# The gathered token tile first through residual and queries, and 352 score columns instead of 384

## The chip, the cores and the metric

The kernel runs on one core of a Trainium2 chip. The metric is the device time of one execution in microseconds. One execution was also recorded by the hardware profiler; all rows below come from that record. PE is TensorE, DVE VectorE, ACT ScalarE, POOL GpSimd and SP SyncE, which here only issues transfers.

## The reference

One encoder block over 512 tokens of 1024 features: a mixer (convolution and pooling heads), a product-key expert layer, and a gated embedding.

```python
h = h + jnp.concatenate([y_conv, y_pool], axis=-1) @ w_o[i]
h = h + peer_ffn(rms_norm(h, g_ffn[i]), w_q[i], sub_keys[i], expert_u[i], expert_v[i])
gate = jax.nn.sigmoid(rms_norm(h, g_ple[i]) @ w_ple_gate[i])
h = h + gate * (p[i] @ w_ple_proj[i])

def peer_block(xb, w_q, sub_keys, expert_u, expert_v):   # xb: normed tokens
    q = (xb @ w_q).reshape(T, PEER_HEADS, 2, PEER_HALF)
    s = jnp.einsum('thpd,hpkd->thpk', q, sub_keys)
    sv, si = lax.top_k(s, PEER_TOPK)                      # 16 of 128, per half
    cand = sv[:, :, 0, :, None] + sv[:, :, 1, None, :]    # 256 sums per head
    top_s, pos = lax.top_k(cand.reshape(T, 8, 256), PEER_TOPK)
    gate = jax.nn.softmax(top_s)
    act = jax.nn.gelu(jnp.einsum('thkd,td->thk', expert_u[eidx], xb))
    return jnp.einsum('thk,thkd->td', gate * act, expert_v[eidx])
```

Each token uses 8 x 16 = 128 of 16384 experts; an expert has a row of 1024 floats in U and one in V.

## The kernel before, in words

The 512 tokens are four tiles of 128. Every fp32 operand is split into a high part (ACT, a copy to fp32r) and a low part (DVE, source minus high part), and each product is three matmuls (high·high, high·low, low·high: `mm3`, lines 118 to 127).

The expert layer works in two ways. The last tile (`ND`, the gathered tile) fetches the 128 U rows and 128 V rows of each token by indirect DMA on POOL (line 536; one gather brings one row for each of 128 tokens), multiplies and sums on DVE (lines 556, 560). The other three tiles (the dense ones, 384 columns) are scored against all experts: 128 U blocks of 128 experts, `score` at line 609, with a gate matrix that is zero except at the chosen experts and that PE builds from one-hot rows (`onehot`, lines 447 to 482), then a product with the 128 V blocks (`mix`).

The stages in time: mixer with w_in; residual, where four 1 MB pieces of w_o (256 columns) each serve four tiles (lines 304 to 316); norm and transposes; queries, eight 1 MB pieces of w_q each for 512 columns, followed by key scores and the first top-16 (`head`, lines 498 to 521); phase 1, U blocks 0 to 75 with the remaining top-k work, the one-hots and the first gathers (lines 626 to 640); the fused stage, where U blocks 76 to 127 are scored beside the first V mixes; the last stage with V mixes and the remaining gathers; and a tail with the embedding gate.

What sets the order: up to the end of phase 1 the framework schedules each engine's queue from its own model of durations. `MAIN_ORDER` orders the top-k tasks of the tiles in phase 1, `spent` spreads them evenly over the blocks (line 636), `G_START` and `G_RATE1` (line 640) set from which block and at what rate gathers run there. The later stages are written out by hand, with `RATES` and the rest of the gathers spread over the last stage (line 801). Pieces of weights use two buffers each for the raw load, the high part and the low part (`wraw`, `wH`, `wL`, lines 159 to 170); each loop loads and splits the next piece before it uses the present one. Each engine and each DMA queue runs in its own order.

## Time and profile before

| | us |
|---|---|
| median of 3 runs | 1453.2 (1452.3 to 1453.3) |
| profiled execution | 1454.46 |
| its span (first to last instruction) | 1452.7 |
| PE busy | 1430.8 |
| DVE busy | 1137.7 |
| ACT busy | 614.5 |
| POOL busy | 390.7 |

The profiled execution is longer than its span by 1.8 us, the time around the first and the last instruction. A busy time is the union of an engine's instructions, so overlapped matmuls are counted once. [...]

### The profile page before, as it was taken

The page shows a single profiled execution, that of the slowest core. Times are in us where ns is not written, and L with a number is a line of the kernel's source. Part 1 is how long each engine was busy: PE and PEld are TensorE (multiplying, and loading weights), DVE is VectorE, ACT ScalarE, POOL GpSimd, SP SyncE. Part 2 cuts the span into 40 slices and gives each one's busy share as a digit, 9 for nine tenths or more (in the row PEclk, how much of TensorE's full clock was granted, in tenths as well). Part 3 has the DMA queues.
Part 4 walks back from the last instruction along what each step waited for, and adds up shares of the span by engine and source line. Part 5 has one row for each costly group of instructions (what it writes and reads, how often), then busy time and mean ns, then how long its engine had stood idle before and what let it go on. Part 6 is the DMA issues. An engine that isn't in the chain of part 4 may idle for free.

```text
span 1452.7 us, 20601 instructions
## 1 busy us (share of the span) xinstructions
PE 1430.8 (98%) x7785; PEld 1271.6 (88%) x7785; DVE 1137.7 (78%) x2078; ACT 614.5 (42%) x864; POOL 390.7 (27%) x260
## 2 busy tenths in 40 slices
PE   8999999999998999999999999999999999999997
PEld 5789888999998999998999999999998888788886
DVE  5644579899998987879988778888877777776765
ACT  5321533344564665664333333333333334433354
POOL 0000000002132132125766555454443123342000
PEclk9999999999998999999999999999999999999999
DMA  8223730047688899899998999998997899998721
GB/s 302 87 90 104 242 116 30 30 164 279 227 285 268 274 316 326 262 317 347 380 349 323 375 329 339 347 339 324 346 336 273 317 334 333 335 342 324 249 70 73
DMA packets 152083, 381.38 MB, mean 263 GB/s; under 512 B 10928, under 2 KB 72112, under 8 KB 151728
## 3 DMA queue, kind: packets, MB, share of 16 engines
q1 hardware_dynamic: 72400, 211.75, 41.3%
q0 software_dynamic: 36864, 134.23, 25.3%
q10 hardware_dynamic: 42720, 34.08, 7.2%
q8 instruction: 61, 1.00, 0.3%
q14 instruction: 38, 0.31, 0.1%
HBM read 339.92 MB, written 40.11 MB: 262 GB/s over the span
## 4 chain that ended last, share of the span: by engine, by line
PE 71%; DVE 12%; DMA 7%; issue 6%; ACT 2%; POOL 1%; ACTq 1%; SPq 0%; DVEq 0%; POOLq 0%
PE o L127 11%; PE o L123 11%; PE o L125 11%; PE acc L125 6%; PE acc L123 6%; PE acc L127 6%; PE u L127 5%; PE u L123 5%; PE u L125 5%; DMA uraw<-in_u_blk 3%; DVE uL L586 2%; DMA tH<-in_w_gate 2%; POOL gr L536 1%; PE acc L191 1%; PE tp L516 1%
## 5 line engine op out<-in xcount | busy, mean ns | idle before, releaser
L536 POOL DMA_INDIRECT gr<-in_u_rows,eidx x128 | 201.1, 1571 | 652.5 <-DVE tsm L390 334.6
L536 POOL DMA_INDIRECT gr<-in_v_rows,eidx x128 | 189.4, 1480 | 285.2 <-DVE xrow L560 274.5
L125 PE MATMUL o<-vL,wH 128*128 128x512 f32 x768 | 237.2, 390 | 0.7 <-DVE vL L604 0.7
L123 PE MATMUL o<-vH,wH 128*128 128x512 f32 x768 | 237.7, 390 | 0.3 <-ACT wH L685 0.3
L127 PE MATMUL o<-vH,wL 128*128 128x512 f32 x768 | 237.3, 390 | 0.1
L598 ACT ACTIVATE vH<-vraw 128x1024 fp32r<-128x1024 f32 x128 | 135.4, 1058 | 218.3 <-PE o L127 160.8
L123 PE MATMUL acc<-xH,uH 128*128 128x384 f32 x608 | 206.6, 340 | 3.4 <-ACT uH L580 3.4
L604 DVE TENSOR_TENSOR vL<-vraw,vH 128x1024 fp32r<-128x1024 f32 x128 | 156.2, 1221 | 65.2 <-ACT vH L598 64.9
L125 PE MATMUL acc<-xL,uH 128*128 128x384 f32 x608 | 206.8, 340 | 0.0
L127 PE MATMUL acc<-xH,uL 128*128 128x384 f32 x608 | 204.7, 339 | 0.2 <-DVE uL L586 0.2
L580 ACT ACTIVATE uH<-uraw 128x1024 fp32r<-128x1024 f32 x128 | 135.3, 1058 | 100.6 <-DMA uraw<-in_u_blk 64.0
L586 DVE TENSOR_TENSOR uL<-uraw,uH 128x1024 fp32r<-128x1024 f32 x128 | 155.7, 1217 | 24.8 <-ACT uH L580 24.8
L125 PEld LDWEIGHTS o<-vL,wH 128*128 128x128 f32 x768 | 144.0, 188 | 32.3 <-DVE vL L604 1.5
L127 PEld LDWEIGHTS o<-vH,wL 128*128 128x128 f32 x768 | 143.9, 188 | 31.2 <-DVE wL L690 1.0
L560 DVE SCALAR_TENSOR_TENSOR xrow<-gr,gate,xrow 128x1024 f32<-128x1024 f32 x128 | 164.1, 1282 | 5.1 <-DMA xrow<-h_d 4.6
L123 PEld LDWEIGHTS o<-vH,wH 128*128 128x128 f32 x768 | 143.3, 188 | 27.2 <-ACT wH L685 0.7
L556 DVE SCALAR_TENSOR_TENSOR gr<-gr,xrow 128x1024 f32<-128x1024 f32 x128 | 154.3, 1218 | 4.2 <-DMA gr<-in_u_rows,eidx 4.1
L127 PE MATMUL u<-xH,uL 128*128 128x384 f32 x416 | 139.6, 336 | 0.0
L123 PE MATMUL u<-xH,uH 128*128 128x384 f32 x416 | 139.5, 335 | 0.0
L125 PE MATMUL u<-xL,uH 128*128 128x384 f32 x416 | 139.3, 335 | 0.0
L123 PEld LDWEIGHTS acc<-xH,uH 128*128 128x128 f32 x608 | 115.4, 190 | 4.1 <-ACT uH L580 4.1
L127 PEld LDWEIGHTS acc<-xH,uL 128*128 128x128 f32 x608 | 115.1, 189 | 0.8 <-DVE uL L586 0.8
(214 smaller groups left out, 2336.8 us busy)
## 6 DMA issues: line engine op xcount, KB each, us to landing
uraw<-in_u_blk SPq DMA_DIRECT2D x128, 512.0 KB, 5.2
vraw<-in_v_rows SPq DMA_DIRECT2D x128, 512.0 KB, 6.0
G_d<-stage ACTq DMA_DIRECT2D x12, 1664.0 KB, 12.8
gq<-G_d SPq DMA_DIRECT2D x26, 768.0 KB, 7.0
A_d<-a ACTq DMA_DIRECT2D x17, 768.0 KB, 6.0
aq<-A_d SPq DMA_DIRECT2D x17, 768.0 KB, 9.5
wraw<-in_w_in SPq DMA_DIRECT2D x8, 1024.0 KB, 5.8
wraw<-in_w_q SPq DMA_DIRECT2D x8, 1024.0 KB, 5.8
```

The costliest lines, as they stand in the source:

```text
L123: nc.tensor.matmul(ps, lh, rh, start=start, stop=False)
L125: nc.tensor.matmul(ps, lh, rl, start=False, stop=False)
L127: nc.tensor.matmul(ps, ll, rh, start=False, stop=stop)
L191: nc.tensor.matmul(ps, pT[:, c, t * P:(t + 1) * P], wp[hf][:, c], start=c == 0, stop=c == 1)
L516: nc.tensor.matmul(ps[:, o:o + P], qb[b][:, t * P:(t + 1) * P], keys[:, 2 * hd + b], start=True, stop=True)
L536: nc.gpsimd.indirect_dma_start(out=g, out_offset=None, in_=table, in_offset=bass.IndirectOffsetOnAxis(ap=eidx[:, k:k + 1], axis=0))
L556: ins = nc.vector.scalar_tensor_tensor(g, g, 1.0, xrow, op0=OP.mult, op1=OP.mult, accum_out=act[:, k:k + 1])
L560: ins = nc.vector.scalar_tensor_tensor(accg, g, gate3[:, k - P:k - P + 1], accg, op0=OP.mult, op1=OP.add)
L580: nc.scalar.activation(ublk[i][1], ublk[i][0], AF.Copy)
L586: nc.vector.tensor_tensor(ublk[i][2], raw, uh.bitcast(F32), op=OP.subtract)
L598: nc.scalar.activation(vblk[n][1], vblk[n][0], AF.Copy)
L604: nc.vector.tensor_tensor(vblk[n][2], raw, vh.bitcast(F32), op=OP.subtract)
```

## The change

The gathered tile goes through residual and queries alone and first. Its four pieces of w_o are loaded and split; then eight q pieces for it alternate with four o pieces for the three dense tiles; then eight q pieces come for the dense tiles. So 12 o and q pieces become 24 (`todo_w`). The low part of the last seven is made on GpSimd (`eng`). The top-k tasks of the gathered tile run in that stage instead of phase 1.

Scores take 352 columns (`TU`) instead of 384. The last 32 tokens of tile 2 get their scores from gathered U rows: 32 more gathers (`XK`), each of 32 tokens x 4 rows, on indices that four small POOL DMAs lay over 128 partitions (`index_x`). Their activations go back by four more DMAs (`actt`) and into the gate of tile 2 before its one-hots (`weigh_x`), with one scale per token (`unit_x`) that the eviction of these tokens' one-hots on DVE takes off again. The score tiles hold 1.0 in the last 32 columns. The gathers of the fused stage keep their rates; phase 1 has 64 instead of 46, the last stage 60 instead of 46.

```diff
-G_START = 10
-G_RATE1 = 0.7
+G_START = 4
+G_RATE1 = 0.9
-MAIN_ORDER = ((ND, 0, 99), (0, 0, 99), (1, 0, 99), (2, 0, 99))
+MAIN_ORDER = ((2, 0, 14), (0, 0, 99), (1, 0, 99), (2, 14, 99))
+XT = 32
+XQ = P // XT
+XK = P // XQ
+TU = TD - XT
-    iotar = consts.tile([P, 2 * OB // PR, P, PR], F16, name="iotar")
+    iotar = consts.tile([P, 2, P * PR], F16, name="iotar")
-    def split_ld(src, hi, lo):
+    def split_ld(src, hi, lo, eng=None):
         nc.scalar.activation(hi, src, AF.Copy)
-        nc.vector.tensor_tensor(lo, src, hi.bitcast(F32), op=OP.subtract)
+        (eng or nc.vector).tensor_tensor(lo, src, hi.bitcast(F32), op=OP.subtract)
+        def index_x():
...
+            for q in range(XQ):
+                nc.gpsimd.dma_start(eidx_x[q * XT:(q + 1) * XT], ex[XROWS, q * XK:(q + 1) * XK])
+        def weigh_x():
+            while todo["x"]:
+                gather(1, True)
+            g = d["g"][XROWS]
+            nc.vector.tensor_tensor(g, g, act_t[XROWS], op=OP.mult)
...
+            nc.gpsimd.dma_start(unit_d.rearrange("a n -> n a"), s)
+            nc.gpsimd.dma_start(unit_x, bass.AP(tensor=unit_d.tensor, offset=unit_d.offset, ap=[[0, P], [1, XT]]))
+                if t0 >= TU:
...
+                        nc.vector.tensor_tensor(o.rearrange("p i t -> p t i"), pv[:, :, i], unit, op=OP.mult)
+    todo_w = ([("o", n) for n in range(4)] + [("o", 0), ("q", 0), ("q", 1), ("o", 1), ("q", 2), ("q", 3), ("o", 2),
+              ("q", 4), ("o", 3), ("q", 5), ("q", 6), ("q", 7)] + [("q", hd) for hd in range(H)])
+    NX = len(todo_w) - H
+    def weights(n):
+        m = n + 1
+        if m < len(todo_w):
+            kind, i = todo_w[m]
+            got[m] = piece(w_o if kind == "o" else w_q, i * 256, 2 if kind == "q" and m < NX else 1,
+                           nc.gpsimd if m > NX else None)
+        return got.pop(n)
+    for n in range(4):
+        residual(weights(n), n, [ND])
...
+    for n in range(4, NX):
+        w = weights(n)
+        kind, i = todo_w[n]
+        if kind == "o":
+            residual(w, i, range(ND))
+        else:
+            queries_n(w, i)
...
     for hd in range(H):
+        both = projT(weights(NX + hd), xh, xl, TD)
...
+        for _ in range(3):
+            if tasks_n:
+                tasks_n.pop(0)[1]()
+        for t in (2, 0, 1):
+            heads[t](hd, s[:, t])
+        for kind, n in (("x", XK if ready else 0), ("u", P), ("v", P)):
...
-            mm3(ps[:, :TD], uh[:, c], ul[:, c], xh[:, c, :TD], xl[:, c, :TD], c == 0, c == DC - 1)
+            mm3(ps[:, :TU], uh[:, c], ul[:, c], xh[:, c, :TU], xl[:, c, :TU], c == 0, c == DC - 1)
```

The first place is the queue of SP from the w_o pieces to the last w_q piece. Before (`wraw` is a raw weight piece, `uraw` a raw U block):

```order
L160 DMA wraw<-in_w_o 128x8x256 x4
L160 DMA wraw<-in_w_q 128x8x256 x3
L327 DMA h_d<-h 128x1024 x3
L325 DMA keys<-in_keysT 128x2048
L327 DMA h_d<-h 128x1024
L193 DMA ple_d<-pleo 128x512 x2
L160 DMA wraw<-in_w_q 128x8x256
L193 DMA ple_d<-pleo 128x512 x2
L574 DMA uraw<-in_u_blk 128x1024 x2
L334 DMA xs<-in_g_ffn 128x1024
L574 DMA uraw<-in_u_blk 128x1024 x3
L160 DMA wraw<-in_w_q 128x8x256 x4
```

After, from the keys of the gathered tile (`uH<-in_keysT`) on; three rows with w_o and one with `ple_d` stand ahead of it:

```order
L550 DMA uH<-in_keysT 128x1024 x2
L174 DMA wraw<-in_w_o 128x8x256
L174 DMA wraw<-in_w_q 128x8x256
L547 DMA h_d<-h 128x1024
L553 DMA xs<-in_g_ffn 128x1024
L174 DMA wraw<-in_w_q 128x8x256
L174 DMA wraw<-in_w_o 128x8x256
L174 DMA wraw<-in_w_q 128x8x256 x2
L174 DMA wraw<-in_w_o 128x8x256
L174 DMA wraw<-in_w_q 128x8x256
L174 DMA wraw<-in_w_o 128x8x256
L174 DMA wraw<-in_w_q 128x8x256 x3
```

Twelve pieces that each served all four tiles are now followed or preceded by twelve more; o and q pieces alternate, and the keys, the row store `h_d` and the gain vector stand between them.

The second place is DVE in phase 1, around U block 50. Before (`uL` is the low part of a U block, `oh` and `gg` a one-hot pair, `gr` a gathered row's product):

```order
L586 TENSOR_TENSOR uL<-uraw,uH 128x1024
L460 TENSOR_TENSOR gg<-oh,tr 128x2048
L586 TENSOR_TENSOR uL<-uraw,uH 128x1024
L556 SCALAR_TENSOR_TENSOR gr,act<-gr,xrow 128x1024
L458 TENSOR_TENSOR oh<-iotar,tr 128x2048
L460 TENSOR_TENSOR gg<-oh,tr 128x2048
L556 SCALAR_TENSOR_TENSOR gr,act<-gr,xrow 128x1024
L458 TENSOR_TENSOR oh<-iotar,tr 128x2048
L586 TENSOR_TENSOR uL<-uraw,uH 128x1024
L556 SCALAR_TENSOR_TENSOR gr,act<-gr,xrow 128x1024
L460 TENSOR_TENSOR gg<-oh,tr 128x2048
L586 TENSOR_TENSOR uL<-uraw,uH 128x1024
```

After, at the rows of `weigh_x` (`tgx`, `xhi`, `xlo`, `xs`, `xr`):

```order
L434 TENSOR_TENSOR tgx<-tgx,actt 32x128
L709 TENSOR_TENSOR uL<-uraw,uH 128x1024
L471 TENSOR_TENSOR oh<-iotar,tr 128x2048
L435 TENSOR_REDUCE xhi<-tgx 32x1
L436 TENSOR_REDUCE xlo<-tgx 32x1
L471 TENSOR_TENSOR oh<-iotar,tr 128x2048
L474 TENSOR_TENSOR gg<-oh,tr 128x2048
L679 SCALAR_TENSOR_TENSOR gr,act<-gr,xrow 128x1024
L437 SCALAR_TENSOR_TENSOR xs_6140<-xlo,xhi 32x1
L474 TENSOR_TENSOR gg<-oh,tr 128x2048
L679 SCALAR_TENSOR_TENSOR gr,act<-gr,xrow 128x1024
L438 TENSOR_SCALAR xs_6140<-xs_6140 32x1
```

The small rows of the gate of the last 32 tokens now lie among the one-hot pairs and gathers, and in these twelve rows stands one U split where there were four.

## Rows read from the trace of the kernel before

**Rows 1.** The page, span and part 1: busy us (share) xinstructions of each engine.
```profile
span 1452.7 us, 20601 instructions
...
PE 1430.8 (98%) x7785; PEld 1271.6 (88%) x7785; DVE 1137.7 (78%) x2078; ACT 614.5 (42%) x864; POOL 390.7 (27%) x260
```

**Rows 2.** The page, part 4: shares of the chain that ended last, by engine.
```profile
PE 71%; DVE 12%; DMA 7%; issue 6%; ACT 2%; POOL 1%; ACTq 1%; SPq 0%; DVEq 0%; POOLq 0%
```

**Rows 3.** Windows by stage: length, busy us of each engine, PEclk, DMA share, GB/s.
```profile
114.10:160.30 46.20, 46.20 (x386) 46.20 (x385) 20.34 (x37) 12.46 (x15) 0.00 (x0) 1.00 0.34 109
...
171.00:274.00 103.00, 103.00 (x509) 85.51 (x508) 85.47 (x449) 33.09 (x44) 0.00 (x0) 1.00 0.25 80
274.00:651.90 377.90, 372.76 (x2615) 363.06 (x2615) 340.08 (x751) 219.36 (x358) 77.15 (x52) 0.99 0.79 262
651.90:1092.00 440.10, 440.10 (x2212) 398.78 (x2212) 366.12 (x407) 158.15 (x190) 235.09 (x159) 1.00 0.93 344
1092.00:1362.00 270.00, 268.89 (x1192) 222.47 (x1191) 202.73 (x197) 101.63 (x114) 78.20 (x46) 1.00 0.89 323
```

**Rows 4.** Timeline of PE, residual: start, us of one, engine, line, operation.
```profile
118.03 0.28 PE L123 MATMUL acc<-wH,mixH 128*128 128x256 f32 x1
...
120.67 0.28 PE L123 MATMUL acc<-wH,mixH 128*128 128x256 f32 x1
```

**Rows 5.** Timeline of PE, scores of U blocks.
```profile
497.14 0.33 PE L127 MATMUL acc<-xH,uL 128*128 128x384 f32 x1
...
500.09 0.33 PE L127 MATMUL acc<-xH,uL 128*128 128x384 f32 x1
```

**Rows 6.** Timeline of PE, queries; x2 is two matmuls in one row.
```profile
177.28 0.63 PE L123 MATMUL acc<-xH,wH 128*128 128x512 f32 x2
...
183.35 0.63 PE L125 MATMUL acc<-xL,wH 128*128 128x512 f32 x2
```

**Rows 7.** Timeline of ACT and DVE: the split of one w_o piece.
```profile
148.83 1.91 ACT L96 ACTIVATE wH<-wraw 128x2048 fp32r<-128x2048 f32 x1 [9.55 <-PE acc L127]
...
150.77 2.29 DVE L97 TENSOR_TENSOR wL<-wraw,wH 128x2048 fp32r<-128x2048 f32 x1 [1.53 <-ACT wH L96]
```

**Rows 8.** DMA issues: transfer, queue, count, KB each, us from issue to landing.
```profile
wraw<-in_w_q SPq DMA_DIRECT2D x8, 1024.0 KB, 5.8
```

**Rows 9.** Windows of 448 to 452, columns as in rows 3.
```profile
448.00:450.00 2.00, 0.00 (x0) 0.00 (x0) 1.66 (x4) 0.76 (x1) 1.81 (x1) 0.98 0.85 348
450.00:452.00 2.00, 1.31 (x6) 0.95 (x7) 1.67 (x2) 2.00 (x6) 0.07 (x1) 0.50 0.92 297
452.00:454.00 2.00, 2.00 (x17) 1.91 (x16) 1.01 (x2) 1.55 (x4) 0.00 (x0) 0.50 1.03 385
```

**Rows 10.** Windows by blocks 4–19, 20–39, 40–59, 60–75 of phase 1.
```profile
281.90:353.40 71.50, 71.50 (x414) 71.50 (x414) 70.70 (x338) 29.49 (x41) 9.75 (x7) 1.00 0.59 211
353.40:450.30 96.90, 93.78 (x662) 90.73 (x660) 94.05 (x193) 56.67 (x91) 25.86 (x15) 1.00 0.79 258
450.30:560.00 109.70, 107.83 (x797) 103.86 (x798) 93.37 (x107) 71.91 (x124) 25.48 (x17) 0.95 0.90 296
560.00:651.90 91.90, 91.75 (x695) 89.08 (x694) 76.76 (x80) 57.52 (x100) 16.06 (x13) 1.00 0.87 289
```

**Rows 11.** Lines by form: busy us, mean ns of one, idle time before them.
```profile
L586 DVE TENSOR_TENSOR uL<-uraw,uH 128x1024 fp32r<-128x1024 f32 x128 | 155.7, 1217 | 24.8 <-ACT uH L580 24.8
L556 DVE SCALAR_TENSOR_TENSOR gr<-gr,xrow 128x1024 f32<-128x1024 f32 x128 | 154.3, 1218 | 4.2 <-DMA gr<-in_u_rows,eidx 4.1
...
L460 DVE TENSOR_TENSOR gg<-oh,tr 128x2048 f16<-128x2048 f16 x48 | 58.5, 1220 | 0.5
L458 DVE TENSOR_TENSOR oh<-iotar,tr 128x2048 f16<-128x2048 f16 x48 | 58.4, 1221 | 6.2 <-PE g L471 6.1
```

**Rows 12.** Timeline of DVE, two splits in one row.
```profile
437.29 2.31 DVE L586 TENSOR_TENSOR uL<-uraw,uH 128x1024 fp32r<-128x1024 f32 x2
```

**Rows 13.** Window of the fused stage.
```profile
689.70:726.00 36.30, 36.30 (x183) 32.80 (x182) 33.98 (x48) 12.97 (x16) 28.44 (x18) 1.00 1.00 379
```

**Rows 14.** The page, part 5: gathers on POOL.
```profile
L536 POOL DMA_INDIRECT gr<-in_u_rows,eidx x128 | 201.1, 1571 | 652.5 <-DVE tsm L390 334.6
```

## The prediction

> **What bounds the kernel now.** I read the page's sums first: PE is busy for 1430.8 of 1452.7 us, DVE for 1137.7 [rows 1]. A share of 98% says that the kernel is worth what PE has to do, but it is an average, and the chain of waits puts only 71% on PE and 12% on DVE [rows 2]. So I went on to windows by stage: the reader is to see that PE has no gap in the residual, the queries and the fused stage, waits 5.1 us in phase 1, and that other engines are near their own limit in two places: DVE with 340.1 of 377.9 us in phase 1, and the DMA engines with a share of 0.93 in the fused stage [rows 3]. Then I took the distance between starts in timelines, since that is what a matmul costs in a stream: 22 matmuls of 256 columns start in 2.64 us, 0.120 each [rows 4]; 17 of 384 in 2.95, 0.1735 each [rows 5]; 26 of 512 in 6.07, 0.2335 each [rows 6]. These lie on a line, which puts 352 columns at 0.160. Last come the windows of phase 1 by blocks, which show where DVE has room and where it has none [rows 10].

> **Columns.** A U block is scored by 8 x 3 = 24 matmuls, so the change takes 24 x 0.0134 = 0.32 us from a block: 24.4 us from the 76 blocks of phase 1 and 16.7 us from the 52 of the fused stage, 41 us of PE work in all. The bound from the other side is nothing: no row has 352 columns, and they could cost what 384 do. The 256-column row speaks against that, and I take the line.

> **Front stage: +27 us.** PE's work in residual and queries stays as it was: the residual has the same matmuls, and of the queries 384 x 0.1735 plus 192 x 0.120 = 89.7 us stand for 384 x 0.2335 = 89.7. About 2 us are added for the gathered tile's own transposes and key scores. What changes is the supply. A piece is now used for 24 x 0.120 = 2.9 us where it serves one tile, for 8.6 us where it serves three in the residual, and for 48 x 0.1735 = 8.3 us in the later queries. Its split takes 1.91 us on ACT and after it 2.29 us on DVE, 4.2 us together [rows 7]. With two buffers for the parts, the split of the next piece can begin only when the last piece's matmuls are over, that is beside the present ones. Beside 8.6 us it is hidden, beside 2.9 us it isn't: 1.3 us are missing. By `todo_w` twelve pieces are split beside a one-tile piece (those behind each of the four first o pieces and behind each of the eight q pieces): 12 x 1.3 = 16 us. The halves in which the q pieces are split would hide about one of these microseconds each, and I count that against the semaphores and the transfer behind it. Raw pieces too have two buffers: a transfer lands 5.8 us after its issue [rows 8] and holds the buffer until the split is over, 10.0 us for two pieces or 5.0 each, against 4.2 by the split alone. That counts where one-tile pieces follow each other, the four o at the start and q5 to q7 at the end: 7 or 8 x 0.8 = 6 us. On SP the keys and the row store stand ahead of the second w_o pieces, and on DVE the low parts share the queue with the first top-16 of the gathered tile; for both I put 3 us. 16 + 6 + 3 + 2 = 27. The lower bound is 2 us, if everything but PE's work is covered; the upper one is 12 x 5.8 = 70 us, if no landing is hidden.

> The reloads don't load the DMA engines much (12 MB more where they are busy to a share of 0.25 to 0.34 [rows 3]). From the eighteenth piece on, the low part is made on GpSimd. The trace has no arithmetic on POOL. The nearest row is the same split on DVE, 2.3 us; four times that is 9.2. It is hidden while it stays under the 8.3 us of a three-tile piece less 1.9 on ACT, 6.4 us; at 9.2 us seven pieces would cost 7 x 2.8 = 20 us. I take nothing, by the row it is nearest to. [...]

> **Phase 1: 0 us.** PE loses 24.4 us of work here; what has to be asked is whether DVE lets it run ahead. DVE loses the decode of the gathered tile's top-k, which moves to the queries (about 18 us), and gets 18 more gathers, 64 for 46, at 1.22 + 0.08 us, of which 1.2 are left when they follow closely (two splits take 2.31 us in one row [rows 12]): +21. Sixteen one-hot evictions come to it from ACT, about +5. So its sum goes from 335 us in these windows to about 343 [rows 10], while PE's goes from 365 to 342. The engines would be level, and they are not so in each place. By the order, blocks 20 to 39 hold 99 us of DVE work against 89 of PE. Blocks 40 to 59 hold five more one-hots and about five more gathers than before: 5 x 2.3 [rows 11] + 5 x 1.2 = 18, to 112 us of DVE against 101 of PE, where the window now takes 109.7. Only blocks 4 to 19 and 60 to 75 give PE its gain, some 5 + 10 us. If each window took the larger of the two sums, phase 1 would be 11 us shorter; but before, DVE at 94.1 of 96.9 us and PE at 93.8 already lost 3.1 us to waits between them [rows 10], and with both at the limit for 200 us I expect the rest to be lost likewise. I take 0, with −24 us if DVE hides everything and +15 us if DVE reaches no more than 0.95 in the middle windows (112 / 0.95 = 118, 99 / 0.95 = 104: 8 + 7 more than now).

> In front of the one-hots of tile 2 stands a chain: the last of the 32 gathers, the gelu, four POOL DMAs, ten small DVE rows, two more DMAs. POOL runs in order and has five gathers of 1.57 us [rows 14] ahead of a DMA, about 8 us. The one-hots of tiles 0 and 1, over 70 us of DVE work, lie beside it: nothing, and up to 5 us if DVE's queue is held by the wait, for the U splits stand behind it in the same queue. The smaller `iotar` is read with a repeated axis; its row of 1.22 us [rows 11] stays as long as that form keeps its rate. If it took twice as long, the 48 one-hots would cost 48 x 1.2 = 59 us of DVE; the operand `tr` is already read with repeated axes, so I take nothing.

> **Fused stage: −14 us.** PE is busy for the whole of the 440.1 us [rows 3], so 16.7 us of its work are time. Against it stands the DMA share of 0.93, and 1.00 with 379 GB/s in a stretch of 36 us [rows 13]: a stage shorter by 4% moves the same U and V blocks and the same 164 gathers. Where the share is 1.00 PE can't get faster; I give back a sixth, 2.7 us. Bounds: −16.7 and 0.

> **Last stage: +2 us.** Fourteen more V gathers are 14 x 0.5 MB = 7.3 MB, 23 us at the 323 GB/s of this stage, beside 270 us with a share of 0.89 [rows 3]; 240 + 23 still go in, tightly. DVE has 67 us to spare for 14 x 1.3. Bounds 0 and +10.

> **The sum.** 27 + 0 − 14 + 2 = +15. The profiled execution took 1454.5 us around its span of 1452.7, 1.3 more than the median of the runs, 1453.2; 1454.5 + 15 is 1469.5, and on the median's footing 1468.

> **The rivals.**
> A: the gain arrives. The split and the transfers of one-tile pieces are covered but for 8 us (the halves of the q pieces make it so), DVE keeps up in phase 1 with three quarters of its gain, −18 us, and the fused stage gives −16: −26, 1427 us, between 1412 and 1442. For it speaks that DVE's sum of 343 us would fit into PE's new 342; against it the 70.7 of 71.5 us for which DVE is busy in blocks 4 to 19 [rows 10] and the splits' 4.2 us.
> B: the clock. After PE had waited for all of 448 to 450 us, the granted clock was 0.50, the lower of its two levels, from 450 to 454 [rows 9]. If the repeated waits in the front stage do the same, one-tile pieces run at half speed, 5.8 us: the wait of 22 us in my sum is replaced by 12 x 2.9 = 35, and pieces of three tiles behind them start slow, some 2 us each on eight: 27 becomes 56, and the time about 1496. Against it: my single waits are shorter than those 2.9 us. [...]
> C: the terms cancel. With phase 1 at −11 by its window sums and the front stage at +22, the sum is −1: within 0.2%.
> D: 352 columns cost what 384 do, against [rows 4 to 6]. Then the fused stage gains nothing and phase 1 carries its added DVE work: 27 + 10 + 3, 1493 us.

> **How the numbers follow.** Forecast 0.48, A 0.29, B 0.12, C 0.06, D 0.05. The likeliest case's own range is 1453 to 1488: the front stage between 15 and 45 us, phase 1 between −11 and +12. The range of 8 in 10 takes in the upper half of A and most of B and D: 1425 to 1500. What can be told from no change here is about 0.2%, 2.9 us. Faster by more than that are nearly all of A (0.28) and 0.05 of the forecast's lower end: 0.33. Within it lie C and 0.02 of the forecast: 0.08. Slower: 0.41 of the forecast, B, D and 0.01 of A: 0.59.

> **What would show it.** In the profile after: the distance of starts in U blocks is 0.160 us. Between the end of the mixer and the first U block PE waits about 25 us, in gaps of 1 to 3 us ended by ACT or DVE of `wH` and `wL`, each behind a one-tile piece, at a granted clock near 1.00; a clock near 0.5 there is B. Phase 1 takes about 378 us again with DVE over 0.9 of it in blocks 20 to 59 and PE waiting for `uL`; if it takes 360 with PE at 98%, A is right. The fused stage takes some 426 us. The forecast is wrong if PE's waits in the front stage stay under 10 us, or if phase 1 shrinks by more than 12.

## The result

The changed kernel takes 1494.7 us as the median of four runs (1489.3 to 1501.2), against 1453.25 us (1452.3 to 1455.3): a ratio of 1.0285, 95% interval 1.0243 to 1.0328. It is slower by 41 us, where +15 was forecast. The profiled run is the shortest of the four, 1489.34 us around a span of 1487.6; what follows explains its 34.9 us over the profiled run of before. The other runs are 5 to 12 us longer again, at a lower mean granted clock of PE (0.981 to 0.984 against 0.987); no trace shows where.

The page after, to be held against [rows 1, 2]: span, busy times, shares of the chain.

```profile
span 1487.6 us, 21344 instructions
...
PE 1414.5 (95%) x7993; PEld 1259.8 (85%) x7993; DVE 1217.3 (82%) x2190; ACT 625.9 (42%) x900; POOL 468.4 (31%) x324
...
PE 63%; DVE 18%; DMA 9%; ACT 5%; issue 4%; ACTq 0%; SPq 0%; POOL 0%; DVEq 0%; POOLq 0%
```

PE is busy for 16 us less and the span is 35 us longer. In the chain, PE went from 71% to 63%, DVE from 12% to 18%, ACT from 2% to 5%: PE waits more. I cut the span at the first U score, at the first score of the fused stage and at its last. These are the windows after (columns as in [rows 3]), the first from 114 us, the last to the end:

```profile
114.00:305.27 191.27, 171.26 (x1140) 162.77 (x1139) 158.10 (x569) 81.54 (x122) 32.94 (x9) 0.95 0.51 163
305.27:694.35 389.08, 358.82 (x2615) 342.52 (x2614) 357.56 (x765) 205.35 (x342) 105.28 (x80) 0.99 0.82 276
694.35:1127.90 433.55, 433.55 (x2274) 393.49 (x2275) 375.19 (x431) 158.46 (x191) 250.55 (x176) 1.00 0.95 358
1127.90:1487.60 359.70, 344.52 (x1528) 280.14 (x1527) 264.62 (x315) 140.10 (x182) 79.46 (x55) 0.99 0.75 278
```

And those of before, cut at the same events:

```profile
114.00:273.31 159.31, 158.86 (x929) 136.95 (x929) 112.25 (x495) 52.74 (x68) 0.00 (x0) 1.00 0.33 106
273.31:651.89 378.58, 373.44 (x2618) 363.74 (x2617) 340.77 (x755) 220.01 (x359) 77.14 (x52) 0.99 0.79 262
651.89:1103.93 452.04, 452.04 (x2274) 409.98 (x2274) 375.00 (x414) 160.58 (x192) 241.74 (x165) 1.00 0.92 342
1103.93:1452.70 348.77, 339.67 (x1528) 279.97 (x1527) 248.12 (x301) 140.98 (x182) 71.57 (x41) 0.99 0.73 265
```

| stage | before | after | difference | forecast |
|---|---|---|---|---|
| front, to the first U score | 273.3 | 305.3 | +32.0 | +27 |
| phase 1 | 378.6 | 389.1 | +10.5 | 0 |
| fused stage | 452.0 | 433.6 | −18.5 | −14 |
| last stage and tail | 348.8 | 359.7 | +10.9 | +2 |

The column term came as computed. In the stream of a U block (timeline of PE after) 21 distances span 3.38 us, 0.161 each, against 0.160 forecast from [rows 4 to 6]:

```profile
305.27 0.32 PE L134 MATMUL acc<-xH,uH 128*128 128x352 f32 x1
...
308.65 0.32 PE L134 MATMUL acc<-xH,uH 128*128 128x352 f32 x1
```

In the front PE waited for 20.0 us, before for 0.5. Its waits (engine, tile that PE writes, releaser: us in total, times, longest):

```profile
PE tp L619 <- ACT s L622: 6.1, 1, 6.1
PE tp L570 <- ACT qn L567: 5.5, 2, 5.2
PE acc L134 <- ACT wH L107: 3.7, 4, 1.6
PE acc L136 <- DVE ms L126: 1.7, 1, 1.7
PE acc L136 <- DVE wL L108: 1.6, 2, 1.4
```

The waits that I had forecast, for parts of a piece (`wH`, `wL`), are 5.3 us and not 22; with the one put down to `ms`, a small row beside which the low part that PE needed was finished, they are 7.0. Two single waits, behind the copies of scores (`s`) and queries (`qn`), are as large as all of them, each. PE's busy time in the front grew by 12.4 us too, of which new work is 1.8 (16 transposes of 0.11); most of the rest, by my estimate 191.3 x 0.05 = 9.6, is the clock, 0.95 in the mean of the stage:

```profile
130.00:140.00 10.00, 6.71 (x46) 6.31 (x45) 6.21 (x7) 5.05 (x6) 0.00 (x0) 0.88 1.01 308
150.00:160.00 10.00, 7.62 (x51) 6.48 (x51) 5.64 (x8) 6.39 (x13) 0.00 (x0) 0.91 0.33 106
210.00:220.00 10.00, 5.35 (x22) 4.35 (x23) 7.01 (x17) 7.09 (x10) 1.70 (x1) 0.66 0.69 236
240.00:250.00 10.00, 3.91 (x18) 3.58 (x17) 9.93 (x11) 3.24 (x6) 5.68 (x2) 0.68 0.65 203
```

A clock of 0.66 and 0.68 stands beside the two long waits, 0.88 and 0.91 in the windows with the short ones. At 138.2 us, behind two waits of 1.6 and 1.7 us, the 256-column matmuls start every 0.21 us, at 141.2 every 0.12 as in [rows 4]. Such waits don't always lead to it: in dve_lo (below) they were 1.3 and 1.7 us at the same place, and the starts behind them stayed 0.12 us apart.

Phase 1 by the same cuts as [rows 10]:

```profile
320.00:382.80 62.80, 61.34 (x370) 60.94 (x371) 61.21 (x254) 26.20 (x35) 2.04 (x4) 0.97 0.54 179
382.80:488.10 105.30, 95.81 (x702) 91.26 (x701) 97.81 (x191) 57.27 (x95) 31.35 (x22) 1.00 0.81 279
488.10:611.60 123.50, 109.17 (x865) 102.11 (x865) 115.34 (x142) 73.53 (x136) 48.97 (x35) 0.97 0.98 325
611.60:694.35 82.75, 79.15 (x598) 75.15 (x595) 68.48 (x82) 42.05 (x68) 17.13 (x13) 1.00 0.86 284
```

The outer two windows are 9 us shorter each (62.8 for 71.5, 82.8 for 91.9); the middle two are 8.4 and 13.8 us longer, DVE busy for 97.8 of 105.3 and 115.3 of 123.5 us, the DMA engines at 0.98 in the second. That leaves 4 of the 10.5 us; the other 6 lie ahead of the first window. There, from the first U score on, 14.7 us pass with DVE busy throughout, before 8.6 (after, then before):

```profile
305.27:320.00 14.73, 13.36 (x87) 13.07 (x86) 14.73 (x104) 6.31 (x10) 5.78 (x6) 1.00 0.61 215
273.31:281.90 8.59, 8.59 (x57) 8.58 (x56) 5.90 (x39) 4.43 (x6) 0.00 (x0) 1.00 0.00 0
```

PE's waits in phase 1 add up to 30.3 us. I had expected waits for `uL`; these are 9.1 us. 12.1 us end with ACT's evictions of the one-hot products (`stage`) and 8.2 us with ACT's high parts of U (`uH`).

The longest wait of the front, the 6.1 us for `s`, has this history (timelines of POOL, DVE, ACT and PE after, in this order):

```profile
236.63 9.06 POOL L108 TENSOR_TENSOR wL<-wraw,wH 128x2048 fp32r<-128x2048 f32 x2 [13.75 <-ACT wH L107]
...
237.02 0.33 DVE L366 MAX8 tts<-tt 128x8 f32<-128x50 f32 x2
...
238.72 2.61 DVE L389 CAST tpf<-tpos 128x128 f16<-128x128 uint32 x1
241.25 4.59 DVE L372 TENSOR_TENSOR tts<-tts,tmx 128x128 f32<-128x128 f32 x1
...
245.87 0.31 ACT L373 ACTIVATE tts<-tts 128x128 f32<-128x128 f32 x1 [4.62 <-DVE tts L372]
246.09 0.85 ACT L622 ACTIVATE s<-tp 128x512 f32<-128x512 f32 x2
...
246.72 0.79 PE L619 MATMUL tp<-keys,yb 128*128 128x128 f32 x2 [6.09 <-ACT s L622]
```

GpSimd splits two pieces one after the other from 236.63 to 245.7, about 4.5 us each. DVE's MAX8 rows run on beside it. The cast of 128 elements per partition then takes 2.61 us, and the subtraction in front of the Exp 4.59: each ends within 0.15 us of the end of a split on GpSimd. ACT's Exp waits for that subtraction, ACT's copy of the scores stands behind the Exp, and PE waits 6.09 us for the copy. Before, the same two operations took 0.29 and 0.27 us (lines by form, behind the first bar busy us and the mean in ns):

```profile
L384 DVE TENSOR_TENSOR tts<-tts,tmx 128x128 f32<-128x128 f32 x4 | 1.1, 286 | 0.0
...
L401 DVE CAST tpf<-tpos 128x128 f16<-128x128 uint32 x4 | 1.1, 269 | 0.0
```

The same is seen at six of the seven splits: rows of `tmul` took 4.62 and 4.22 us and one of `tij` 4.24, each ending within 0.6 us of the end of a split; a `uL` took 3.44 and ended 1.1 us, about its own time, behind one.

### The profile page after: what moved, and what is told of

Same layout as the page of the kernel before. It is cut to its first block, busy times and chain, and to the rows that moved or that the text cites. A ratio compares the mean times of both kernels' runs of the same rounds, so it can differ in the third digit from the quotient of the medians.

```text
span 1487.6 us, 21344 instructions
## 1 busy us (share of the span) xinstructions
PE 1414.5 (95%) x7993; PEld 1259.8 (85%) x7993; DVE 1217.3 (82%) x2190; ACT 625.9 (42%) x900; POOL 468.4 (31%) x324
## 4 chain that ended last, share of the span: by engine, by line
PE 63%; DVE 18%; DMA 9%; ACT 5%; issue 4%; ACTq 0%; SPq 0%; POOL 0%; DVEq 0%; POOLq 0%
PE o L138 10%; PE o L134 10%; PE o L136 10%; PE acc L138 6%; PE acc L136 6%; PE acc L134 6%; PE u L134 5%; PE u L138 5%; PE u L136 5%; DMA tH<-in_w_gate 3%; DMA uraw<-in_u_blk 3%; DVE uL L709 2%; DVE xrow L675 2%; DVE gr L679 1%; ACT stage L496 1%
## 5 line engine op out<-in xcount | busy, mean ns | idle before, releaser
L644 POOL DMA_INDIRECT gr<-in_u_rows,eidx x128 | 194.9, 1523 | 229.1 <-DVE gr L679 193.4
L644 POOL DMA_INDIRECT gr<-in_v_rows,eidx x128 | 183.6, 1434 | 258.7 <-DVE xrow L675 248.5
L134 PE MATMUL acc<-xH,uH 128*128 128x352 f32 x608 | 201.4, 331 | 8.2 <-ACT uH L703 8.2
L138 PE MATMUL acc<-xH,uL 128*128 128x352 f32 x608 | 200.0, 332 | 9.2 <-DVE uL L709 9.1
L136 PE MATMUL acc<-xL,uH 128*128 128x352 f32 x608 | 198.5, 326 | 0.0
L709 DVE TENSOR_TENSOR uL<-uraw,uH 128x1024 fp32r<-128x1024 f32 x128 | 158.0, 1236 | 16.5 <-ACT uH L703 14.7
L134 PEld LDWEIGHTS o<-vH,wH 128*128 128x128 f32 x768 | 143.0, 189 | 30.5 <-ACT wH L812 4.8
L134 PE MATMUL u<-xH,uH 128*128 128x352 f32 x416 | 134.9, 324 | 0.7 <-ACT a L758 0.7
L138 PE MATMUL u<-xH,uL 128*128 128x352 f32 x416 | 134.3, 323 | 0.0
L136 PE MATMUL u<-xL,uH 128*128 128x352 f32 x416 | 134.0, 322 | 0.0
L138 PEld LDWEIGHTS acc<-xH,uL 128*128 128x128 f32 x608 | 115.8, 191 | 12.4 <-DVE uL L709 12.1
L134 PEld LDWEIGHTS acc<-xH,uH 128*128 128x128 f32 x608 | 116.2, 191 | 10.7 <-ACT uH L703 10.6
```

The source lines that it names most:

```text
L134: nc.tensor.matmul(ps, lh, rh, start=start, stop=False)
L136: nc.tensor.matmul(ps, lh, rl, start=False, stop=False)
L138: nc.tensor.matmul(ps, ll, rh, start=False, stop=stop)
L644: nc.gpsimd.indirect_dma_start(out=g, out_offset=None, in_=table, in_offset=bass.IndirectOffsetOnAxis(ap=idx[:, k:k + 1], axis=0))
L709: nc.vector.tensor_tensor(ublk[i][2], raw, uh.bitcast(F32), op=OP.subtract)
```

## The experiments

All ratios are against the kernel before, run on the same chip. Stage lengths are those of the profiled run, cut as above.

| run | ratio (95% interval) | first U score | phase 1 | fused | rest |
|---|---|---|---|---|---|
| the change | 1.0285 (1.0243 to 1.0328) | 305.3 | 389.1 | 433.6 | 359.7 |
| cols384 | 1.0331 (1.0282 to 1.0379) | 304.7 | 383.0 | 452.2 | 359.0 |
| front_only | 1.0239 (1.0208 to 1.0270) | 303.8 | 383.3 | 452.2 | 351.0 |
| cols_only | 1.0103 (1.0056 to 1.0150) | 273.1 | 408.1 | 433.7 | 355.2 |
| topk_late | 1.0289 (1.0258 to 1.0320) | 305.4 | 392.0 | 435.6 | 362.3 |
| dve_lo | 1.0128 (1.0109 to 1.0147) | 297.5 | 378.8 | 436.2 | 361.2 |
| queue | 1.0317 (1.0292 to 1.0343) | 302.8 | 394.6 | 433.5 | 364.7 |
| x_no_mult | 1.0308 (1.0269 to 1.0347) | 305.0 | 403.7 | 433.6 | 369.2 |
| x_no_fetch | 1.0197 (1.0180 to 1.0215) | 307.9 | 383.7 | 434.7 | 360.7 |
| gp_before | 1.0005 (0.9985 to 1.0025) | 273.0 | 378.9 | 452.0 | 350.7 |
| front_dve | 1.0188 (1.0153 to 1.0224) | 297.0 | 376.2 | 452.2 | 353.0 |
| last46 | 1.0113 (1.0084 to 1.0141) | 299.2 | 378.6 | 439.9 | 350.0 |
| dve_lo_queue | 1.0181 (1.0152 to 1.0210) | 297.5 | 382.2 | 435.0 | 359.8 |
| x_thin | 1.0168 (1.0141 to 1.0194) | 296.3 | 388.4 | 433.6 | 361.2 |
| x_no_fetch2 | 1.0121 (1.0091 to 1.0152) | 300.1 | 378.1 | 434.6 | 361.7 |
| x_none | 0.9971 (0.9957 to 0.9986) | 298.9 | 359.9 | 434.1 | 363.0 |
| dve_cols384 | 1.0319 (1.0284 to 1.0355) | 298.3 | 391.2 | 452.2 | 360.1 |

### The two halves of the change

**cols384.**

```diff
-            mm3(ps[:, :TU], uh[:, c], ul[:, c], xh[:, c, :TU], xl[:, c, :TU], c == 0, c == DC - 1)
+            mm3(ps[:, :TD], uh[:, c], ul[:, c], xh[:, c, :TD], xl[:, c, :TD], c == 0, c == DC - 1)
```

> The changed kernel with all 384 columns scored again; the gathers of the last 32 tokens and all else stay, the extra 32 columns are computed and not used. PE gets 24 x 0.0135 = 0.32 us back in each of 128 U blocks, 41 us in all. Theory (phase 1 is bound by DVE, the fused stage by PE): the fused stage grows by 15 to 18 us, phase 1 by 0 to 8, nothing elsewhere: 1510 to 1520 us. Rival (PE bounds both stages): +41, 1535 us. Rival (352 columns are no cheaper than 384): 1495 us.

The fused stage grew by 18.7 us, phase 1 did not grow: the columns were worth 18.7 us in one stage and nothing in the other. The total, 0.5% above the change, is below what the theory said, and the intervals overlap.

**front_only.**

```diff
-TU = TD - XT
+TU = TD
...
-G_START = 4
-G_RATE1 = 0.9
+G_START = 10
+G_RATE1 = 0.7
...
-MAIN_ORDER = ((2, 0, 14), (0, 0, 99), (1, 0, 99), (2, 14, 99))
+MAIN_ORDER = ((0, 0, 99), (1, 0, 99), (2, 0, 99))
...
-    NGATHER = XK + 2 * P
-    todo = {"x": XK, "u": P, "v": P}
+    NGATHER = 2 * P
+    todo = {"x": 0, "u": P, "v": P}
```

> The changed front alone: the gathered tile first with 24 pieces, its top-k tasks in the queries stage; scores with 384 columns, no gathers for the last 32 tokens, 46 gathers in phase 1 as before. Theory (the front costs 32 us by waits and clock, and a PE-bound phase 1 can give back no more than the 5 us that PE waited there): first U score 32 us later than before, 1480 to 1486 us. Rival (DVE, relieved of some 18 us of top-k in phase 1, gives the delay back): 1465 to 1470 us. Rival (the front is not what costs): within 5 us of before, 1450 to 1458.

The front alone costs 2.4%, most of the loss, and its delay of 30.5 us is not given back. Phase 1 is even 4.7 us longer than before, though DVE is busy for only 329.7 us there, against 340.8; that the theory did not have, and the total, 1492.0 us, is above its range.

**cols_only.**

```diff
-G_START = 4
-G_RATE1 = 0.9
+G_START = 8
+G_RATE1 = 0.95
...
-MAIN_ORDER = ((2, 0, 14), (0, 0, 99), (1, 0, 99), (2, 14, 99))
+MAIN_ORDER = ((2, 0, 14), (ND, 0, 99), (0, 0, 99), (1, 0, 99), (2, 14, 99))
...
+    for qd in range(4):
...
+        for t in range(NT):
...
```

> The front of before (every piece of w_o and w_q serves four tiles) with 352 columns and the 32 gathers for the last 32 tokens; the top-k of the gathered tile in phase 1, after the first tasks of tile 2; gathers from block 8 at 0.95 a block. Theory: the first U score comes at 273 us as before; the fused stage gains 17 to 18 us, the last stage loses up to 11 to 14 more gathers, phase 1 loses 0 to 15 since DVE gets 26 us more to do there: 1446 to 1462 us. Rival (the loss of the change sits in the gathers and the chain of the 32 tokens, not in the front): 1475 us or more.

No delay in the front, −18 us in the fused stage, +6 in the last: as expected. But phase 1, which holds all the top-k work and the 64 gathers, lost 30 us and not 0 to 15:

```profile
273.09:681.20 408.11, 363.36 (x2618) 350.11 (x2617) 366.24 (x809) 208.84 (x345) 103.07 (x78) 0.95 0.80 269
```

DVE is busy for 366 us there, against 340.8 before; PE waits 45 us. What of this is DVE's work and what the transfers, this run doesn't show. The total lies between theory and rival: the columns by themselves don't pay either.

### The Exp and the queue

**topk_late.**

```diff
-G_START = 4
-G_RATE1 = 0.9
+G_START = 8
+G_RATE1 = 0.95
...
-MAIN_ORDER = ((2, 0, 14), (0, 0, 99), (1, 0, 99), (2, 14, 99))
+MAIN_ORDER = ((ND, 0, 99), (2, 0, 14), (0, 0, 99), (1, 0, 99), (2, 14, 99))
...
-        for _ in range(3):
-            if tasks_n:
-                tasks_n.pop(0)[1]()
```

> The changed kernel with the top-k tasks of the gathered tile back in phase 1 (first in its list; gathers from block 8 at 0.95). Theory: the 6.1 us wait of PE behind the Exp on ACT in the queries stage goes, with 2 to 4 us of low clock after it, so the first U score comes 8 to 10 us earlier, near 296 us; phase 1, bound by DVE, gets back the 18 us of these tasks: 1495 to 1505 us. Rival (phase 1 isn't bound by DVE): 1483 to 1488 us.

A miss by its design: the framework schedules the tasks as soon as their data are there, so the Exp stood at the same place (at 245.38 us) and PE waited its 6.1 us again. The place in the program text did not decide.

**queue.**

```diff
-                nc.sync.dma_start(h_d[t], h[:, t])
+                nc.gpsimd.dma_start(h_d[t], h[:, t])
...
-    nc.sync.dma_start(keys, keysT)
+    nc.gpsimd.dma_start(keys, keysT)
```

> The changed kernel with the stores of the three dense tiles' rows and the load of the keys on GpSimd's DMA queue instead of SP's, so that the w_q pieces behind them on SP don't wait for the residual and for the release of the mixer's memory. Theory (the 5.2 us wait of PE at 209 to 214 us is a late w_q piece, behind which ACT's eviction of the queries stands): that wait goes, with about 2 us of low clock after it; first U score near 298 us, total 1484 to 1491 us. Rival (the piece is late by the weight buffers or the DMA rate, not by the queue): unchanged within 2 us there, 1492 to 1500 us.

The late piece did come from SP's queue: the wait for `qn` fell from 5.5 to 1.9 us. But the first U score came only 2.4 us earlier, other waits took its place, and the total did not fall. **dve_lo_queue** has the same edit on top of the next one.

> All low parts on DVE, and the row stores of the dense tiles and the keys on GpSimd's DMA queue. With GpSimd's splits gone from that queue, the stores and the keys stand behind nothing there. Theory (the 5.7 us wait behind the late w_q piece is the next thing in the front): first U score 292 to 295 us, total 1468 to 1474 us. Rival (another wait takes its place, as with the queue alone, where 4 of 5 us came back): first U score 296 to 298, 1474 to 1480 us.

The rival held. The `qn` wait was 2.3 us instead of 6.0, and the first U score came at 297.5 us as in dve_lo. The transposes of the dense tiles waited instead, for DVE (waits of PE in the front):

```profile
PE acc L134 <- ACT wH L107: 3.0, 3, 1.4
PE tp L570 <- ACT qn L567: 2.3, 2, 1.9
...
PE tp L148 <- DVE xL L151: 1.6, 1, 1.6
PE g L148 <- DVE xs L169: 1.5, 1, 1.5
```

### GpSimd's splits

**dve_lo.**

```diff
-                           nc.gpsimd if m > NX else None)
+                           None)
```

> The changed kernel with the low parts of the last seven w_q pieces on DVE instead of GpSimd. In the changed kernel two DVE rows beside GpSimd's split took 4.6 and 2.6 us where the same operations took 0.29 and 0.27 before, and ACT's Exp and PE waited behind them for 6.1 us. Theory (GpSimd's arithmetic holds DVE up): these rows are short again, the 6.1 us and some 2 us of low clock behind them go, DVE gets 7 x 2.3 = 16 us of work and loses about as much in stalls; first U score near 297 us instead of 305, total 1482 to 1490 us. Rival (the wait comes from the Exp and the DVE rows being slow on their own, or DVE is full without GpSimd): first U score at 303 to 308, 1493 to 1502 us.

The cast and the subtraction are short again (timeline of DVE of this run):

```profile
246.07 0.25 DVE L389 CAST tpf<-tpos 128x128 f16<-128x128 uint32 x1
246.24 0.28 DVE L372 TENSOR_TENSOR tts<-tts,tmx 128x128 f32<-128x128 f32 x1
```

PE's wait of 6.1 us behind them is gone. The first U score came at 297.5 us, 7.8 earlier; phase 1 took 378.8 us, 10.3 less:

```profile
114.00:297.47 183.47, 169.27 (x1140) 161.51 (x1140) 150.60 (x562) 81.59 (x122) 0.41 (x2) 0.96 0.52 170
297.47:676.23 378.76, 352.94 (x2614) 340.91 (x2613) 354.89 (x772) 207.06 (x342) 102.39 (x78) 0.99 0.83 282
676.23:1112.39 436.16, 434.34 (x2273) 393.23 (x2274) 379.32 (x438) 158.03 (x191) 252.79 (x179) 1.00 0.95 357
1112.39:1473.60 361.21, 344.41 (x1529) 278.60 (x1527) 264.52 (x316) 139.68 (x182) 94.52 (x55) 1.00 0.75 278
```

In ratios the edit takes 1.0285 to 1.0128, more than half of the loss; in the profiled runs 14.0 us (1487.6 to 1473.6), since the two later stages are 4.1 us longer. The theory held, and its size was too small: I had counted nothing for phase 1. A part of it is the backlog with which DVE enters: the stretch of 14.7 us behind the first U score takes 11.0 here. How the rest arises, no run separates. **front_dve** is the same edit on front_only.

> The changed front alone (384 columns, no rows for the last 32 tokens, 46 gathers in phase 1), and the low parts of the last seven w_q pieces on DVE. Theory (GpSimd's splits cost some 8 us in the front and 5 to 10 in phase 1 whatever the columns): first U score near 297 us, total 1.0 to 1.8% over before, 1470 to 1482 us. Rival (what GpSimd costs comes only with the 64 gathers of the changed phase 1): the front gains 8, phase 1 nothing, 1483 to 1488 us.

6.8 us in the front and 7.1 in phase 1, without columns and without the gathers of the last 32 tokens: the splits cost that by themselves. The profiled runs differ by 12.0 us; the ratios, 1.0239 and 1.0188, differ by less, and their intervals overlap a little. 1.0188 is just above what was expected.

**gp_before.**

```diff
...
-            pieces["q%d" % (hd + 1)] = piece(w_q, (hd + 1) * 256)
+            pieces["q%d" % (hd + 1)] = piece(w_q, (hd + 1) * 256, nc.gpsimd)
...
```

> The kernel before with one edit: the low parts of w_q pieces 1 to 7 on GpSimd instead of DVE. DVE loses 7 x 2.3 = 16 us of work. Theory (while GpSimd computes, DVE's two-operand and cast rows stand still): seven splits of 4.6 us each hold DVE up in a stage where it is busy for 85 of 103 us; the queries or the first blocks of phase 1 get longer, 1458 to 1472 us, with single DVE rows of 2 to 5 us that took 0.3 to 1.2. Rival (no contention, the stalls in the changed kernel had another cause): DVE is relieved by 16 us in the queries, 1448 to 1455 us.

Seven splits on GpSimd in the kernel before cost nothing and bring nothing. The theory as worded fell; its mechanism did not. Beside six of the seven stood only MAX8, FIND_INDEX8, MATCH_REPLACE8 and their loads on DVE. Beside the first stood the rows of the norm, and one of them, of one element per partition, took 2.77 us and ended with the split (timelines of POOL and DVE of this run):

```profile
162.00 4.51 POOL L97 TENSOR_TENSOR wL<-wraw,wH 128x2048 fp32r<-128x2048 f32 x1 [161.55 <-ACT wH L96]
...
163.75 2.77 DVE L105 SCALAR_TENSOR_TENSOR nt<-r,ms 128x1 f32<-128x1 f32 x1
```

So it matters what DVE has to do beside GpSimd. In the changed kernel that is, above all, the decode of the gathered tile's top-k, which the change itself had moved there. The rows of the changed kernel differ by operation: TENSOR_TENSOR (4.59 us for 0.29) and CAST (2.61 for 0.27) were held, MAX8 was not (two in 0.33 us beside a split, as ahead of it), nor was a SCALAR_TENSOR_TENSOR of `xL` (0.60 us at 220.0 us beside a split, 0.60 at 231.1 without one). What makes the difference, no run here shows.

### What binds phase 1

**x_no_mult.** The rows for the last 32 tokens are fetched and not multiplied.

```diff
...
-            else:
+            elif kind != "x":
...
                 row, a = (xrow_x, act_x) if kind == "x" else (xrow.rearrange("p (c n) -> p c n", c=DC), act)
...
```

> The changed kernel in which the 32 gathered rows of the last 32 tokens are fetched, but not multiplied on DVE (their activations are a constant): DVE loses 32 x 1.2 = 38 us in phase 1, the DMA traffic stays. Theory A (phase 1 is bound by DVE): phase 1 shrinks from 389 to 362 to 372 us, 1470 to 1480 us in all. Theory B (the transfers of phase 1 bind, 0.97 of the DMA engines in blocks 40 to 59): phase 1 stays within 5 us, 1490 us or more.

Inconclusive: with nobody to wait for, the rows were fetched in a burst, and the U blocks came late. The window of it:

```profile
398.00:471.00 73.00, 51.15 (x366) 47.05 (x365) 54.20 (x100) 31.08 (x57) 39.27 (x33) 0.86 1.01 387
```

The DMA engines are full at 387 GB/s (a share of 1.01) and PE busy for 51 of 73 us. It doesn't tell DVE from the transfers; it shows what gathers without a pace do to the U blocks.

**x_no_fetch.** Not fetched, but DVE multiplies other data of the same size.

```diff
+        if kind == "x":
+            return g
         nc.gpsimd.indirect_dma_start(out=g, out_offset=None, in_=table,
...
-                ins = nc.vector.scalar_tensor_tensor(gv, gv, 1.0, row, op0=OP.mult, op1=OP.mult,
+                src = gv if kind == "u" else xrow.rearrange("p (c n) -> p c n", c=DC)
+                ins = nc.vector.scalar_tensor_tensor(gv, src, 1.0, row, op0=OP.mult, op1=OP.mult,
```

> The changed kernel in which the 32 rows of the last 32 tokens are not fetched, but DVE multiplies as before, on other data of the same size: 16.8 MB less in phase 1, the DVE work stays. Theory A (phase 1 is bound by DVE): phase 1 stays within 5 us of 389, 1488 us or more. Theory B (the transfers bind): phase 1 shrinks by 12 us or more, below 1484 us in all.

Phase 1 took 383.7 us, 5.4 less: neither theory alone. With the splits off GpSimd I asked again, with three edits on dve_lo. **x_thin** fetches all rows and multiplies 64 of 1024 elements (its edit is shown); **x_no_fetch2** is x_no_fetch on dve_lo; **x_none** leaves out both the fetch and all but 64 elements of the product.

```diff
...
+                if kind == "x":
+                    gv, row = gv[:, :, :8], row[:, :, :8]
```

> The kernel with all low parts on DVE, in which each of the 32 rows for the last 32 tokens is fetched and waited for as before, but DVE multiplies only 64 of its 1024 elements: 32 x 1.1 = 35 us less on DVE in phase 1, the transfers and their pace stay. Theory A (DVE bounds phase 1): 379 us there become 355 to 365, total about 1455 to 1465. Theory B (transfers bound it, 0.99 of the DMA engines in blocks 40 to 59): 374 us or more there, total 1472 or more.

> The kernel with all low parts on DVE, in which the 32 rows for the last 32 tokens are not fetched, while DVE multiplies other data of the same size: 16.8 MB less in phase 1, the DVE work stays. Theory A (DVE bounds phase 1): 374 us or more there. Theory B (transfers bound it): 355 to 365 us there, total 1455 to 1465.

> The same with neither the fetch nor the multiplication of the 32 rows (64 elements of other data are multiplied instead). If either theory alone is right, this is as fast as the right one of the two; if DVE and transfers each bound a part of phase 1, it is faster than both: 350 to 358 us there against 373 us of PE-bound phase 1 with 384 columns less 24.

Phase 1 of the three, one row each, in this order:

```profile
296.29:684.69 388.40, 360.45 (x2614) 346.19 (x2614) 330.45 (x781) 204.87 (x343) 100.01 (x81) 0.96 0.81 280
```

```profile
300.05:678.17 378.12, 351.18 (x2614) 341.00 (x2614) 355.63 (x773) 205.85 (x342) 59.50 (x46) 0.98 0.73 244
```

```profile
298.85:658.72 359.87, 347.95 (x2615) 339.77 (x2614) 325.07 (x773) 205.62 (x342) 54.47 (x46) 0.99 0.75 251
```

Against 378.8 us of dve_lo: without DVE's part 388.4, without the transfers 378.1, without both 359.9. Neither theory alone is right. DVE's busy time falls by 24 us in x_thin and the stage gets longer, the DMA share falls from 0.83 to 0.73 in x_no_fetch2 and it stays; only without both does it get shorter, by 19 us. Each edit also changes the order that the framework works out, which alone may be worth several microseconds here: in x_thin the last of the 32 gathers starts at 486 us, in dve_lo at 513. Why x_thin is 10 us longer stays open. The time is lost in blocks 40 to 59 (135.5 us for 109.7), and PE's waits there are 0.3 us for `uL` and 10.6 for ACT's one-hot evictions. x_none, a little above the 350 to 358 us expected there, says one more thing: with the 32 gathers all but free, the design would gain 0.3%.

**dve_cols384** is the edit of cols384 on dve_lo.

> The kernel with all low parts on DVE and all 384 columns scored again. Theory (the column saving is worth nothing in phase 1 since another engine or the transfers bound it, and 16 to 18 us in the fused stage): phase 1 within 5 us of 379, the fused stage 452, total 1.0 to 1.4% above the kernel with 352, 1490 to 1497 us. Rival (phase 1 becomes PE-bound once GpSimd's splits are gone): phase 1 390 us or more, total 1500 or more.

```profile
298.34:689.49 391.15, 376.81 (x2615) 365.53 (x2614) 361.30 (x781) 206.00 (x343) 104.38 (x81) 0.98 0.82 277
```

The rival held. With the splits off GpSimd the columns are worth 12.4 us in phase 1 and 16.0 in the fused stage, and the total differs by 1.9%. So half of the 24.4 us does arrive in phase 1 here, where with the splits on GpSimd (cols384) nothing of it did; that DVE's stalls had hidden it is argued and not shown.

### The last stage

**last46.**

```diff
-RATES = (1.5, 3.2, 2.9)
+RATES = (1.5, 3.2, 3.29)
...
```

This kernel has the edit of dve_lo as well.

> The kernel with all low parts on DVE, in which the fused stage takes 14 more gathers (3.29 instead of 2.9 a block), so that the last stage has 46 again instead of 60. Theory (the last stage is bound by transfers at a share of 0.9, 14 rows of 0.5 MB take 7 to 11 us there; the fused stage is at 0.95 and pays for them as well): the last stage gets 7 to 10 us shorter, the fused stage 5 to 10 longer, total 1470 to 1478 us. Rival (the fused stage has room, since PE was busy throughout): 1464 to 1469 us.

Fused stage and rest of this run:

```profile
677.83:1117.70 439.87, 436.51 (x2273) 394.62 (x2274) 394.82 (x452) 156.78 (x191) 276.44 (x193) 1.00 0.97 371
1117.70:1467.70 350.00, 340.74 (x1529) 279.72 (x1527) 247.96 (x302) 140.85 (x182) 69.08 (x41) 0.99 0.72 266
```

The rest is 11.2 us shorter than in dve_lo with 60 gathers (361.2) and back at 350.0 as before, 348.8; the fused stage is 3.7 longer at a DMA share of 0.97. The 14 gathers cost 11 us in the last stage and a third of that in the fused stage. Whether as transfers or as DVE work, no run separates: behind the last U score PE waited for 6.4 us in the changed kernel and for 1.0 before, 3.6 of it for DVE's low parts of V and 2.8 for ACT. The total, 1.0113 against 1.0128, is no difference that the intervals bear out.

## Why the prediction was wrong

**The sign was right, the size was not.** The largest error is a term that I set to nothing. Without it, in dve_lo, the front is +24.2 us, phase 1 +0.2, the fused stage −15.9 and the rest +12.4, together +20.9 in the profiled run and 1.0128 as a ratio, some 19 us: near the +15, with the errors of the front and the last stage still in it.

**The split on GpSimd: 0 forecast, 14 us measured in the profiled runs, 23 by the ratios.** I bounded GpSimd's own time, 2.3 to 9.2 us, and it took 4.7 us in the mean, under the 6.4 that I had for it. The step that failed was the next one: "it is hidden while it stays under the 8.3 us of a three-tile piece". I priced it as if it used only its own engine. It held DVE, DVE held ACT, ACT held PE: 7.8 us of the front and 10.3 of phase 1 (dve_lo), 6.8 and 7.1 without the columns and the 32 gathers (front_dve). I did not ask what DVE would run beside it.

**The front, +27 forecast, +32 measured: near by luck, two errors against each other.** The waits for parts of a piece were 5.3 to 7.0 us instead of 22. At the q pieces of the gathered tile, which are split in halves, PE waited 0.5 us for parts; that the halves hid the rest is likely and was not tested. In place of the 22 us stood the late piece behind the keys on SP (5.2 us; I had put 3 for SP and DVE together), the stall by GpSimd (6.1) and the clock (about 10, from a mean of 0.95 over 191 us). That last one was in rival B: its mechanism came, as a clock of 0.66 to 0.91 in the windows with waits of 1.4 to 6.1 us, and its size was a third of what B said (10 of 29 us). That my single waits are shorter than those of [rows 9] did not protect them; the wait there is 2.6 us in the trace, not 2.9. The two levels that B names are in that trace: in windows of 0.5 us from 444 to 460 us the clock is 1.00 or, from 450 to 456.5, 0.50, but for the two windows in which it changes.

**Phase 1, 0 forecast, +10.5 measured.** Blocks 20 to 39 took 8.4 us more and blocks 40 to 59 13.8, where my upper end was 7 and 8: DVE had the work that I had summed (97.8 and 115.3 us for 99 and 112) but reached only 0.93 of both windows and not 0.95. The outer windows gave back 18 us, for the 15 of my sum, and the stretch ahead of them took 6 more, for which my sum had no term. The forecast of no gain holds for the kernel without GpSimd's splits (378.8 to 378.6 of before), but not for the reason I gave: less DVE work alone doesn't shorten it (x_thin), half of the column saving arrives (dve_cols384), and the 32 gathers, with their DVE work and transfers, take more than that back (x_none: 19 us).

**The fused stage, −14 forecast, −18.5 measured.** I gave back 2.7 us to the transfers, and that was the error: the share went from 0.92 to 0.95 and PE stayed busy throughout. Why it is 1.8 us more than the 16.7 of the columns is not shown.

**The last stage, +2 forecast, +10.9 measured.** My own bound was +10. "240 + 23 still go in, tightly" was wrong: last46 shows 11 us for these 14 gathers, about half of the 23 that I had for their bytes. That the transfers are the cause is not shown; the waits that grew end with DVE and ACT.

**The sum.** 32.0 + 10.5 − 18.5 + 10.9 = 34.9 in the profiled run; the median is 6.5 us further away, in runs with a lower mean clock, which no trace here explains.

Rival A fell with the front, C with phase 1, D by the distance of starts. None of the runs beats the kernel before with the whole computation; gp_before equals it, and the best form of the change, last46, is 1.1% slower.

## What to carry to other kernels

Work that is moved to GpSimd is not priced by its own duration alone, but by what DVE has to run beside it: here a TENSOR_TENSOR and a CAST that took 0.29 and 0.27 us before took 4.59 and 2.61 beside splits of about 4.5 us, and two MAX8 took 0.33 us with a split beside them and without. Work that is taken from PE is worth time only where PE is the one that ends last (18.7 us in the fused stage and nothing in phase 1, by cols384); count in each stage what the replacement costs on the other engines, for 14 gathers cost 11 us in the last stage (361.2 us in dve_lo, 350.0 in last46, the DMA share 0.75 and 0.72 with the tail). And an operand that is loaded twice to serve fewer rows each time can cost its waits and, behind them, the clock: here 20 us of waits and some 10 of lower clock, the latter an estimate from a mean of 0.95 over 191 us; of both the splits on GpSimd had a part.
